# Bilinear einsum on one core: a kernel under Tile's own ordering rewritten with its own semaphores, 512-column products and row sums per unit of groups

## The chip, the cores and the metric

The kernel runs on one core of a Trainium2 chip. The metric is the device time in microseconds, taken over several executions of the kernel; lower is better. One execution was also recorded by the hardware profiler, and all times of single instructions below are from that recording, in microseconds from the start of its span.

## The reference

```python
batch, dim_i, dim_j, dim_k = 32, 256, 256, 128      # all float32
def reference(x, y, weight):
    return np.einsum('bi,bj,kij->bk', x, y, weight).astype(np.float32)
```

For each of the 128 output columns k, a 256 x 256 matrix `weight[k]` is multiplied from the left by the rows of x and from the right by the rows of y. The weight is 33.6 MB in float32 and each element of it is used once per batch row; x and y are 32 KB each, and the output is 16 KB.

## The kernel before

**Tiling.** The 128 values of k are taken as 4 (`KK`) times 32 groups (`G`), and the 256 values of i as 32 (`IP`) times 8 (`IC`). A group g holds `weight[kk*32+g]` for the four kk: 1 MB of float32. Its tile has 128 partitions, each one pair (ip, kk), and 8 x 256 columns (ic, j). The stationary operand `xblk[:, ic]` is 128 x 128: it has x for partition (ip, kk) and column (b, kk'), and zero wherever kk and kk' differ. So eight products of 256 columns, one for each ic, summed in PSUM, give the 128 rows (b, kk) of `sum_i x[b,i] weight[k,i,:]` for four k at once. VectorE then multiplies this 128 x 256 result by `y4` (y with each row repeated four times) and sums along j in the same instruction (L148), which gives one column of `acc`, 128 x 32. At the end one DMA writes `acc` to the output.

**Loads.** Group 0 is loaded in float32 by one DMA of SyncE's queue (L50, `w0`) and turned into bfloat16 by two ScalarE copies (L133). x and y are loaded by ScalarE's queue (L44, L46). Groups 1 to 31 are loaded by the POOL queue (L64), which casts float32 to bfloat16 on the way. Group 30 is loaded in two parts and group 31 in four (4, 2, 1 and 1 of the eight ic). Every load has its own tile, so no load waits for a buffer; Tile hands eight semaphores round the loads, and so from the ninth on the issue of a load waits for the landing of the one eight before it.

**Preparation.** GpSimd makes an identity matrix (L71, L72) between two loads. VectorE repeats x (L89, eight copies), TensorE transposes it (L95, eight transposes), and VectorE multiplies it by a mask (L80, L104) to make `xblk`. y is transposed by TensorE (L113), repeated by VectorE (L118), transposed back (L123) and copied to `y4` (L129).

**Order.** Tile takes the instructions of each engine in program order, adds the semaphores, and closes with a wait for everything and two barriers of all engines, with a clearing of semaphores between them. In the profile the opening barrier stands under L169 and the closing ones under L180.

Of the kernel before, what the change touches and what calls it, by code (L numbers as in the profile page):

```python
# [1 line left out]

# [4 lines left out]


@with_exitstack
def kernel(  # L10
    ctx: ExitStack,
    tc: tile.TileContext,
    x: bass.AP,
    y: bass.AP,
    weight: bass.AP,
    out: bass.AP,
):
    nc = tc.nc
    P = 128
    f32 = mybir.dt.float32  # L20
    bf16 = mybir.dt.bfloat16
    mult = mybir.AluOpType.mult
    add = mybir.AluOpType.add

    B, I = x.shape
    _, J = y.shape
    K, _, _ = weight.shape
    KK = P // B
    IP = P // KK
    IC = I // IP  # L30
    G = K // KK
    assert KK * B == P and IP * KK == P and IC * IP == I and G * KK == K

    consts = ctx.enter_context(tc.tile_pool(name="consts", bufs=1))
    wpool = ctx.enter_context(tc.tile_pool(name="wpool", bufs=1))
    psx = ctx.enter_context(tc.tile_pool(name="psx", bufs=1, space=bass.MemoryType.PSUM))
    pso = ctx.enter_context(tc.tile_pool(name="pso", bufs=4, space=bass.MemoryType.PSUM))
    tmps = ctx.enter_context(tc.tile_pool(name="tmps", bufs=2))


    w_v = weight.rearrange("(kk g) (ip ic) j -> g ip kk (ic j)", kk=KK, ic=IC)

    x_sb = consts.tile([B, I], f32)
    nc.scalar.dma_start(out=x_sb, in_=x)  # L44
    y_sb = consts.tile([B, J], f32)
    nc.scalar.dma_start(out=y_sb, in_=y)  # L46


    w0 = consts.tile([P, IC * J], f32)
    nc.sync.dma_start(out=w0, in_=w_v[0])  # L50

    def split(g):
        if g == G - 1:
            return [(0, 4), (4, 6), (6, 7), (7, 8)]
        if g == G - 2:
            return [(0, 4), (4, 8)]
        return [(0, IC)]

    w_tiles = {}

    def load(g):
        for lo, hi in split(g):
            wt = wpool.tile([P, (hi - lo) * J], bf16, name=f"w{g}_{lo}")
            nc.gpsimd.dma_start(out=wt, in_=w_v[g][:, :, lo * J:hi * J])  # L64
            for ic in range(lo, hi):
                w_tiles[g, ic] = wt[:, (ic - lo) * J:(ic - lo + 1) * J]

    load(1)

    ident = consts.tile([P, P], f32)  # L70
    nc.gpsimd.memset(ident, 0.0)  # L71
    nc.gpsimd.affine_select(  # L72
        out=ident, in_=ident, compare_op=mybir.AluOpType.not_equal, fill=1.0,
        base=0, pattern=[[-1, P]], channel_multiplier=1,
    )
    for g in range(2, G):
        load(g)

    mask = consts.tile([P, KK], f32)
    nc.vector.tensor_reduce(  # L80
        out=mask, in_=ident.rearrange("p (ip kk) -> p kk ip", kk=KK),
        axis=mybir.AxisListType.X, op=add,
    )


    x_rep = consts.tile([B, IC, IP, KK], f32)
    x_cols = x_sb.rearrange("b (ip ic) -> b ic ip", ic=IC)
    for ic in range(IC):
        nc.vector.tensor_copy(  # L89
            out=x_rep[:, ic, :, :],  # L90
            in_=x_cols[:, ic, :].unsqueeze(2).to_broadcast([B, IP, KK]),
        )
    xt_ps = psx.tile([P, IC, B], f32)
    for ic in range(IC):
        nc.tensor.transpose(  # L95
            out=xt_ps[:, ic, :],
            in_=x_rep[:, ic, :, :].rearrange("b ip kk -> b (ip kk)"),
            identity=ident[:B, :B],
        )


    xblk = consts.tile([P, IC, B, KK], bf16)
    for kk in range(KK):
        nc.vector.tensor_scalar(  # L104
            out=xblk[:, :, :, kk], in0=xt_ps, scalar1=mask[:, kk:kk + 1],
            scalar2=None, op0=mult,
        )


    JH = J // P  # L110
    yt_ps = psx.tile([P, JH, B], f32)
    for jh in range(JH):
        nc.tensor.transpose(  # L113
            out=yt_ps[:, jh, :], in_=y_sb[:, jh * P:(jh + 1) * P],
            identity=ident[:B, :B],
        )
    yt4 = consts.tile([P, JH, B, KK], f32)
    nc.vector.tensor_copy(  # L118
        out=yt4, in_=yt_ps.unsqueeze(3).to_broadcast([P, JH, B, KK])
    )  # L120
    y4_ps = psx.tile([P, J], f32)
    for jh in range(JH):
        nc.tensor.transpose(  # L123
            out=y4_ps[:, jh * P:(jh + 1) * P],
            in_=yt4[:, jh, :, :].rearrange("p b kk -> p (b kk)"),
            identity=ident,
        )
    y4 = consts.tile([P, J], f32)
    nc.vector.tensor_copy(out=y4, in_=y4_ps)  # L129

    w0b = wpool.tile([P, IC * J], bf16)
    for lo, hi in ((0, IC // 2), (IC // 2, IC)):
        nc.scalar.copy(out=w0b[:, lo * J:hi * J], in_=w0[:, lo * J:hi * J])  # L133
    for ic in range(IC):
        w_tiles[0, ic] = w0b[:, ic * J:(ic + 1) * J]

    acc = consts.tile([P, G], f32)
    for g in range(G):
        ps = pso.tile([P, J], f32)
        for ic in range(IC):  # L140
            nc.tensor.matmul(  # L141
                out=ps,
                lhsT=xblk[:, ic, :, :].rearrange("p b kk -> p (b kk)"),
                rhs=w_tiles[g, ic],
                start=(ic == 0), stop=(ic == IC - 1),
            )
        tmp = tmps.tile([P, J], f32)
        nc.vector.tensor_tensor_reduce(  # L148
            out=tmp, in0=ps, in1=y4, scale=1.0, scalar=0.0,
            op0=mult, op1=add, accum_out=acc[:, g:g + 1],  # L150
        )

    out_v = out.rearrange("b (kk g) -> b kk g", kk=KK)
    nc.sync.dma_start(out=out_v, in_=acc)


# [1 line left out]
_INS = ['x', 'y', 'weight']  # L158
_OUTS = [((32, 128), 'float32')]


# [23 lines left out]
```

## Time and profile before

| | |
|---|---|
| median of 11 runs | 88.02 us (87.87 to 88.26) |
| the profiled execution's own time | 88.03 us |
| its span, first to last instruction | 86.2 us |
| TensorE busy | 53.7 us (62%), mean granted clock 0.743 |
| VectorE busy | 18.6 us (22%) |
| GpSimd busy (nearly all of it the issue of loads) | 19.3 us (22%) |
| read from HBM | 33.62 MB, 390 GB/s over the span |

Busy time is an engine's own work; the difference between the execution's time and its span (1.8 us) lies outside the recorded instructions. PE is TensorE's matmul and PEld its loading of stationary operands. PEclk is the share of full clock that TensorE was granted. A row of the DMA queues names the queue: q0 holds the loads of the POOL queue, q1 and q10 those of SyncE and ScalarE, q8 and q14 fetches of instructions.

### The profile page before, as it was taken

Reading aid. Unit: us, or ns where it says so; the run is one execution under the profiler, and the core shown is the slowest. Engines: PE = TensorE matmul, PEld = TensorE weight load, DVE = VectorE, ACT = ScalarE, POOL = GpSimd, SP = SyncE. Lnnn points to the kernel's source line nnn. Section 1 sums busy time; section 2 is a strip of 40 time slices with the busy share of each in tenths; the row PEclk is TensorE's granted clock in tenths of the full one; section 3 lists DMA queues with packets and bytes.
Section 4 is the critical chain, followed back from the end, with each engine's and each line's share of the span. In section 5 each row is a group of like instructions: output and inputs, shape, how many; then the busy total and the mean of one; then the engine's idle time right before and its main releaser. Section 6 shows DMA issues by size and latency. Waiting matters only on the chain.

```text
span 86.2 us, 743 instructions
## 1 busy us (share of the span) xinstructions
PE 53.7 (62%) x268; PEld 32.0 (37%) x268; DVE 18.6 (22%) x79; ACT 3.3 (4%) x3; POOL 19.3 (22%) x41
## 2 busy tenths in 40 slices
PE   0517974677637882378745777378777773776360
PEld 0416643433413442234434434144443341445120
DVE  0794242022222012221130222220122222212220
ACT  2326000000000000000000000000000000000000
POOL 5980222222112221122222221122222211200000
PEclk9999999555895559755696557955555589579999
DMA  0999999999999999999999999999999999999900
GB/s 19 372 268 213 213 213 213 213 213 213 213 213 213 213 218 213 213 213 213 213 213 215 213 213 213 213 213 213 215 213 213 215 217 215 211 204 210 167 10 8
DMA packets 5427, 17.43 MB, mean 202 GB/s; under 512 B 752, under 2 KB 1200, under 8 KB 5296
## 3 DMA queue, kind: packets, MB, share of 16 engines
q0 software_dynamic: 5040, 16.26, 94.9%
q1 hardware_dynamic: 288, 1.07, 3.4%
q10 hardware_dynamic: 96, 0.07, 0.3%
q8 instruction: 2, 0.03, 0.1%
q14 instruction: 1, 0.01, 0.0%
HBM read 33.62 MB, written 0.02 MB: 390 GB/s over the span
## 4 chain that ended last, share of the span: by engine, by line
DMA 90%; issue 5%; POOL 1%; DVE 0%; PE 0%; POOLq 0%; DVEq 0%
DMA w<-in_weight_dram 90%; POOL w L64 1%; DVE tmp L148 0%; PE ps L141 0%; POOL ident L71 0%; POOLq L180 0%; POOLq L169 0%; DVEq L180 0%
## 5 line engine op out<-in xcount | busy, mean ns | idle before, releaser
L141 PE MATMUL ps<-w,xblk 128*128 128x256 bf16 x248 | 50.0, 368 | 24.4 <-DMA w<-in_weight_dram 24.3
L141 PEld LDWEIGHTS <-xblk 128*128 128x128 bf16 x256 | 30.2, 127 | 46.7 <-DMA w<-in_weight_dram 33.8
L64 POOL DMA_DIRECT2D w<-in_weight_dram x35 | 18.7, 541 | 54.3 <-DMA w<-in_weight_dram 53.5
L148 DVE CUSTOM_DVE_ANT_0 tmp<-ps,y 128x256 f32<-128x256 f32 x32 | 13.6, 425 | 61.6 <-PE ps L141 61.6
L95 PE MATMUL xt_ps<-ident,x_rep 32*128 32x32 f32 x8 | 1.2, 302 | 3.0 <-POOL ident L72 3.0
L141 PE MATMUL ps<-w0b,xblk 128*128 128x256 bf16 x8 | 2.1, 411 | 1.3 <-ACT w0b L133 1.3
L148 DVE DVE_READ_ACCUMULATOR2_ANT acc<- 128x1 f32 x32 | 2.7, 83 | 0.0
L104 DVE TENSOR_SCALAR xblk<-xt_ps,mask 128x256 bf16<-128x256 f32 x4 | 2.5, 773 | 0.1
L95 PEld LDWEIGHTS xt_ps<-ident,x_rep 32*128 32x128 f32 x8 | 1.1, 182 | 3.0 <-POOL ident L72 3.0
L133 ACT CAST w0b<-w 128x1024 bf16<-128x1024 f32 x2 | 2.0, 1043 | 3.0 <-DMA w<-in_weight_dram 3.0
L89 DVE COPY x_rep<-x_sb 32x128 f32<-32x128 f32 x8 | 1.3, 228 | 2.6 <-DMA x_sb<-in_x_dram 2.6
L133 ACT ACT_TABLE_LOAD x1 | 1.3, 1283 | 1.6 <-PEq L169 1.6
L113 PE MATMUL yt_ps<-ident,y_sb 32*128 32x32 f32 x2 | 0.4, 301 | 1.0 <-DMA y_sb<-in_y_dram 1.0
L113 PEld LDWEIGHTS yt_ps<-ident,y_sb 32*128 32x128 f32 x2 | 0.3, 200 | 1.1 <-DMA y_sb<-in_y_dram 1.1
L129 DVE COPY y<-y_ps 128x256 f32<-128x256 f32 x1 | 0.4, 425 | 1.0 <-PE y_ps L123 1.0
L123 PE MATMUL y_ps<-ident,yt 128*128 128x128 f32 x2 | 0.6, 417 | 0.0
L123 PEld LDWEIGHTS y_ps<-ident,yt 128*128 128x128 f32 x2 | 0.4, 226 | 0.1
L118 DVE COPY yt<-yt_ps 128x256 f32<-128x256 f32 x1 | 0.5, 451 | 0.0
L80 DVE TENSOR_REDUCE mask<-ident 128x4 f32<-128x128 f32 x1 | 0.4, 361 | 0.0
L72 POOL TENSOR_SCALAR_AFFINE_SELECT ident<-ident 128x128 f32<-128x128 f32 x1 | 0.3, 319 | 0.1
L71 POOL MEMSET ident<- 128x128 f32 x1 | 0.2, 224 | 0.0
L169 POOL MEMSET const-float32-0.0<- 128x1 f32 x1 | 0.1, 98 | 0.2 <-issue 0.2
(3 smaller groups left out, 0.3 us busy)
## 6 DMA issues: line engine op xcount, KB each, us to landing
w<-in_weight_dram POOLq DMA_DIRECT2D x29, 512.0 KB, 19.4
w<-in_weight_dram SPq DMA_DIRECT2D x1, 1024.0 KB, 5.1
w<-in_weight_dram POOLq DMA_DIRECT2D x3, 256.0 KB, 17.0
w<-in_weight_dram POOLq DMA_DIRECT2D x1, 128.0 KB, 14.0
w<-in_weight_dram POOLq DMA_DIRECT2D x2, 64.0 KB, 10.8
x_sb<-in_x_dram ACTq DMA_DIRECT2D x1, 32.0 KB, 1.8
y_sb<-in_y_dram ACTq DMA_DIRECT2D x1, 32.0 KB, 4.0
out_dram<-acc SPq DMA_DIRECT2D x1, 16.0 KB, 1.4
```

The costliest lines, as they stand in the source:

```text
L64: nc.gpsimd.dma_start(out=wt, in_=w_v[g][:, :, lo * J:hi * J])
L80: nc.vector.tensor_reduce(out=mask, in_=ident.rearrange("p (ip kk) -> p kk ip", kk=KK), axis=mybir.AxisListType.X, op=add,)
L89: nc.vector.tensor_copy(out=x_rep[:, ic, :, :], in_=x_cols[:, ic, :].unsqueeze(2).to_broadcast([B, IP, KK]),)
L95: nc.tensor.transpose(out=xt_ps[:, ic, :], in_=x_rep[:, ic, :, :].rearrange("b ip kk -> b (ip kk)"), identity=ident[:B, :B],)
L104: nc.vector.tensor_scalar(out=xblk[:, :, :, kk], in0=xt_ps, scalar1=mask[:, kk:kk + 1], scalar2=None, op0=mult,)
L113: nc.tensor.transpose(out=yt_ps[:, jh, :], in_=y_sb[:, jh * P:(jh + 1) * P], identity=ident[:B, :B],)
L118: nc.vector.tensor_copy(out=yt4, in_=yt_ps.unsqueeze(3).to_broadcast([P, JH, B, KK]))
L123: nc.tensor.transpose(out=y4_ps[:, jh * P:(jh + 1) * P], in_=yt4[:, jh, :, :].rearrange("p b kk -> p (b kk)"), identity=ident,)
L129: nc.vector.tensor_copy(out=y4, in_=y4_ps)
L133: nc.scalar.copy(out=w0b[:, lo * J:hi * J], in_=w0[:, lo * J:hi * J])
L141: nc.tensor.matmul(out=ps, lhsT=xblk[:, ic, :, :].rearrange("p b kk -> p (b kk)"), rhs=w_tiles[g, ic], start=(ic == 0), stop=(ic == IC - 1),)
L148: nc.vector.tensor_tensor_reduce(out=tmp, in0=ps, in1=y4, scale=1.0, scalar=0.0, op0=mult, op1=add, accum_out=acc[:, g:g + 1],)
```

## The change

Parts, in the order of the program:

- SyncE's and ScalarE's loads (`w0`, x, y) are issued inside the Tile context; then the context is closed. Its closing barriers (two of all engines, one after the other) so run at the start, behind these three issues and ahead of everything else. All further instructions are written in plain order per engine with semaphores that the kernel allocates.
- The loads of the POOL queue have a semaphore each and wait for nothing. Group 30 is one load; group 31 is still four.
- x is repeated by one copy of 1024 elements and transposed by four VectorE transposes of 32 x 32 blocks. y4 comes from one float32 product of y with `spread`, an identity with each column repeated four times.
- The 32 groups are taken in units of 8, 8, 6, 4, 3, 2 and 1. Within a unit the loop over ic is outside and the pairs of groups are inside: one product covers two groups, 512 columns, and a stationary operand is loaded once for all pairs of the unit. Units run over ic upward and downward in turn, so that a unit begins with the operand that the last one ended with.
- For each unit but the last, one VectorE multiply covers all its groups and a second instruction sums the rows. The last unit, group 31 alone, keeps the fused instruction.
- After the output's DMA has been issued, SyncE increments a semaphore on which POOL clears the others, and SyncE waits for the landing and clears the output's own. No barrier of all engines stands at the end.

```diff
+UNITS = (8, 8, 6, 4, 3, 2, 1)
+LAST = ((0, 4), (4, 6), (6, 7), (7, 8))
+BANKS = 8
...
+    for ins in (
+        nc.sync.dma_start(out=w0, in_=w_v[0]).then_inc(s_w0, 16),
+        nc.scalar.dma_start(out=x_sb, in_=x).then_inc(s_x, 16),
+        nc.scalar.dma_start(out=y_sb, in_=y).then_inc(s_y, 16),
+    ):
+        tc.no_tile_sem_insts.add(ins.ins.name)
+    tc.close()
+    tc.compile()
...
+    for g in range(1, G):
+        if g < G - 1:
+            pool.dma_start(out=w_sb[:, g, :], in_=w_v[g]).then_inc(s_w[g - 1], 16)
+        else:
+            for s, (lo, hi) in zip(s_last, LAST):
+                pool.dma_start(
+                    out=w_sb[:, g, lo * J:hi * J], in_=w_v[g][:, :, lo * J:hi * J],
+                ).then_inc(s, 16)
+        if g == 2:
+            pool.memset(ident, 0.0).then_inc(s_pool, 1)
+            pool.affine_select(
...
+    t = done(v.tensor_copy(
+        out=x_rep,
+        in_=x_sb.rearrange("b (ip ic) -> b ic ip", ic=IC).unsqueeze(3)
+        .to_broadcast([B, IC, IP, KK]),
+    )._wait_ge(s_x, 16))
+    for q in range(Q):
+        c = v.transpose(
+            out=xt[q * 32:(q + 1) * 32, :, :],
+            in_=x_rep[:, :, q * IP // Q:(q + 1) * IP // Q, :],
         )
...
+    def product(out, lhsT, rhs, first, last, load):
+        return pe.add_instruction(mybir.InstMatmult(
+            name=nc.get_next_instruction_name(), engine=mybir.EngineType.PE,
+            ins=[pe.lower_ap(rhs), pe.lower_ap(lhsT)], outs=[pe.lower_ap(out)],
+            start_tensor_calc=first, stop_tensor_calc=last,
+            tile_size=(P, P), tile_position=(0, 0), ldweights=load,
+        ))
...
+        up = (len(UNITS) - 1 - u) % 2 == 0
+        order = range(IC) if up else range(IC - 1, -1, -1)
+        for n_ic, ic in enumerate(order):
+            for b, g, n in pairs:
+                waits = []
+                if g == G - 1:
+                    waits = [s for s, (lo, _) in zip(s_last, LAST) if lo == ic]
+                elif n_ic == 0:
+                    waits = [s_w[h - 1] for h in range(max(g, 1), g + n)]
...
+                c = product(
+                    ps[:, b, :n, :], xblk[:, ic, :, :].rearrange("p b kk -> p (b kk)"),
+                    w_sb[:, g:g + n, ic * J:(ic + 1) * J],
+                    first=(n_ic == 0), last=(n_ic == IC - 1), load=(held != ic),
+                )
...
+        if n_g > 1:
+            t = done(v.tensor_tensor(
+                out=prod, in0=sums, in1=y4.unsqueeze(1).to_broadcast([P, n_g, J]), op=mult,
+            )._wait_ge(s_pe, n_pe))
+            freed[bank:bank + n_b] = [t] * n_b
+            done(v.tensor_reduce(
+                out=acc[:, g0:g0 + n_g], in_=prod, axis=AX, op=add,
+            )._wait_ge(s_dve, t))
+        else:
+            done(v.tensor_tensor_reduce(
...
+    sp.dma_start(out=out_v, in_=acc)._wait_ge(s_dve, n_dve).then_inc(s_out, 16)
+    sp.sem_inc(s_fin, 1)
+    pool.wait_ge(s_fin, 1)
+    pool.dma_reset(range(nums[0], nums[-1] + 1))
+    pool.sem_clear(range(nums[0], nums[-1] + 1))
+    sp.wait_ge(s_out, 16)
+    sp.sem_clear(s_out)
```

## The prediction

> **What bounds the kernel now.** I read the slices and the chain of the page first.
>
> ```profile
> PEclk9999999555895559755696557955555589579999
> DMA  0999999999999999999999999999999999999900
> ...
> DMA 90%; issue 5%; POOL 1%; DVE 0%; PE 0%; POOLq 0%; DVEq 0%
> ```
>
> The DMA engines are full from the second slice to the 38th, and the chain that ended last is 90% loads of the weight. Nothing that TensorE or VectorE does between slice 2 and slice 37 can be worth time; only the start (before the engines are full), the rate of the loads, and the end (from the last landing to the last instruction) can. So I looked at these three. The timeline of TensorE gives the rate, because each group of eight products starts when its load lands:
>
> ```profile
> 30.57 1.88 PE L141 MATMUL ps<-w,xblk 128*128 128x256 bf16 x8 [0.55 <-DMA w<-in_weight_dram]
> 34.00 1.05 PE L141 MATMUL ps<-w,xblk 128*128 128x256 bf16 x8 [1.55 <-DMA w<-in_weight_dram]
> 36.35 1.89 PE L141 MATMUL ps<-w,xblk 128*128 128x256 bf16 x8 [1.30 <-DMA w<-in_weight_dram]
> 38.79 1.89 PE L141 MATMUL ps<-w,xblk 128*128 128x256 bf16 x8 [0.55 <-DMA w<-in_weight_dram]
> ```
>
> Loads land 2.44 us apart (1.05 MB read in that time is 430 GB/s), except once: 3.43 us before the group at 34.00. The DMA queues between 31 and 33 us show what happened there:
>
> ```profile
> q0 software_dynamic: 115, 0.41, 102.6%
> q8 instruction: 1, 0.02, 2.9%
> ```
>
> One 16 KB packet of instructions took 2.9% of 16 engines x 2 us, 0.93 us of one engine. A load is complete when the slowest of 16 engines is. The completion increments in the trace show it: those of group 1 come from 7.86 to 8.43, 0.57 us apart; from this packet on one engine is some 1.4 us behind the first. A second such packet (0.97 us, at 71.9) puts another engine behind by 1.3 us. The increments of the last part of group 31 run from 81.76 to 83.15, and the third latest comes at 82.37: without the two packets the last load would land 0.78 us earlier. TensorE's instructions cause them: counted from its first, it has passed about 200 at 31.8 us and about 460 at 71.9, 256 apart. (The Trainium skill, "Runtime: NRT & Kernel Launch", Terms, has the instruction memory refilled in 16 KiB blocks, which are these packets.)
>
> The end, in the timeline and in the closing instructions' rows:
>
> ```profile
> 81.89 1.56 PE L141 MATMUL ps<-w,xblk 128*128 128x256 bf16 x8 [0.70 <-DMA w<-in_weight_dram]
> 83.49 0.42 DVE L148 CUSTOM_DVE_ANT_0 tmp<-ps,y 128x256 f32<-128x256 f32 x1 [1.83 <-PE ps L141]
> 83.84 0.08 DVE L148 DVE_READ_ACCUMULATOR2_ANT acc<- 128x1 f32 x1
> 83.95 0.35 SPq L154 DMA_DIRECT2D out_dram<-acc  x1
> ```
>
> ```profile
> L180 SPq EVENT_SEMAPHORE  x9: 17/28/28, 84.3 to 86.2; - x9
> L180 SPq DRAIN  x3: 7/7/13, 85.5 to 85.8; - x3
> L180 POOLq EVENT_SEMAPHORE_RANGE_CLEAR  x1: 120/120/120, 85.8 to 85.8; - x1
> ```
>
> Last landing 83.15, last product over at 83.46, row sum over at 83.92, output issued at 83.95 and landed at 85.38 (1.43 us), and then two barriers with a clearing between them to 86.25: 0.87 us in which no data moves.
>
> **The change part by part.** The sum is against the profiled execution: 88.03 us, a span of 86.25 and 1.78 outside it. Its time is within 0.01 us of the median, so no correction is needed.
>
> *Closing barriers moved to the start: -0.75 us.* At the end SyncE has left one wait and one clearing. With the price of the clearing there is (0.12 us) the end comes 0.12 us after the output's landing, in place of 0.87. POOL's own clearing is released by the output's issue, 1.43 us before its landing, and is covered by it. At the start the two barriers (each some 0.2 us by the distance of the rows above, 85.5 to 85.7 and 86.0 to 86.2) wait for ScalarE, whose issue of y ends at 1.60. So POOL's first load, issued at 1.24 before, is issued at about 2.1 to 2.7. What hides this: the engines are on `w0` from 2.15 to 5.03, and the first packet of group 1 starts on each engine just as its `w0` ends. POOL needs 0.66 us for the issue: 3.4 at the latest, 1.6 us to spare. All of VectorE's, TensorE's and ScalarE's preparation also moves 0.9 to 2 us; ScalarE waits for `w0` until 5.88 anyway, and the first products wait for group 1.
>
> *Loads without waits: 0.* POOL waits 53.5 us in 27 waits now, and the engines are never short of work meanwhile. Issuing all 34 at once (34 x 0.53 us = 18 us) only lengthens the queue. One load for group 30 in place of two saves some 0.03 us (two 2 KB packets at 0.173 us against one of 4 KB at 0.324).
>
> *Instructions: TensorE 545 to 213 by the order of the built programs.* The second fetch disappears. The first comes at about the 200th instruction, now in the last two units: some 1.2 us after group 30 has landed, when the engines have 0.5 to 1.4 us of work left. It then delays one engine by up to 0.9 us, or comes after that engine's last packet. So group 30 lands at 79.76 (now 80.56), and the last part of group 31 between 82.37 and 83.15.
>
> *Products in units.* Unit 5 (groups 29 and 30) cannot begin its second step before group 30 has landed: eight products of 512 columns. At full clock 256 columns have a pitch of 0.11 us here (eight in 1.05 with the last one's 0.28), so 512 take 0.215: 8 x 0.215 + 0.2 = 1.93, from 79.79 to 81.72. Unit 6 needs 8 x 0.11 more and then waits for its last parts: its last product ends between 82.68 and 83.46, 0.31 after the landing as now. The 206 weight loads saved are hidden now (the pitch is that of the columns alone) and bring nothing.
>
> *Row sums.* New on the path: unit 5's multiply and sum stand ahead of the last row sum on VectorE. The nearest row is L148, 425 ns for 256 elements from PSUM: 512 cost between 0.60 and 0.85; I take 0.70. For the sum, L80's 361 ns for 128 elements (read with a stride of four) bounds it at 1.44 above, L148's rate at 0.60 below; I take 0.70, since it reads without a stride. So VectorE is free at 81.75 + 0.70 + 0.05 + 0.70 = 83.20; the last row sum starts between 83.2 and 83.5, say 83.3, and is over at 83.73. **This eats most of the 0.78 us that the fetches gave back.**
>
> *Preparation of x and y: 0.* Ready at about 9 us instead of 8.4; what waits is unit 0's first step, and its second step waits for group 7 at 23 us.
>
> *Sum:* 83.73 + 0.03 to the issue + 1.43 + 0.12 = 85.31, against 86.25: -0.94. Time 88.03 - 0.94 = **87.1 us**.
>
> **Two rules of the skill weighed.** First the clock. Windows of 3.41 us, as the trace has them:
>
> ```profile
> 66.44:69.86 3.42, 2.87 (x15) 1.65 (x12) 0.43 (x2) 0.00 (x0) 0.69 (x2) 0.50 1.06 212
> 69.86:73.27 3.41, 1.36 (x11) 0.81 (x10) 0.87 (x4) 0.00 (x0) 0.53 (x1) 1.00 1.06 214
> 73.27:76.68 3.41, 2.74 (x13) 1.66 (x13) 0.43 (x2) 0.00 (x0) 0.53 (x1) 0.50 1.05 210
> 76.68:80.09 3.41, 2.17 (x17) 1.31 (x15) 0.86 (x4) 0.00 (x0) 0.00 (x0) 1.00 1.11 209
> 80.09:83.50 3.41, 2.07 (x12) 0.98 (x11) 0.44 (x3) 0.00 (x0) 0.00 (x0) 1.00 0.62 93
> ```
>
> Columns after the window: its length, busy time of PE, PEld, DVE, ACT, POOL, then the granted clock, DMA share and GB/s. Windows at half clock with 80% or more of PE busy (2.87, 2.74 of 3.41) are followed by full clock; a full window with 40% (1.36) is followed by half, one with 64% (2.17) stays full. The skill ("TensorE: Matmul & The Clock Gate", Part 1) has the clock fall only after an idle window of about 3.4 us. By the rule unit 5 runs at full clock, as I took it: the gap before it is at most 2.5 us. By the trace it may not: if unit 4 runs at full clock (done 2.6 us after group 28 lands at 74.85), a window that holds the idle rest is under 50% busy, and unit 5 gets half clock: 8 x 0.427 + 0.2 = 3.6 us, 1.7 more. Working the seven units through with these thresholds for every phase of the windows, the last row sum ends at 83.6 to 84.0 in three of four phases and at up to 84.5 in nine of ten.
>
> Second the port. Six loads issued at 2.92 took 3.25 us together, 0.54 each, the same as alone (527 ns), while VectorE's SBUF copies ran beside them (2.60 to 3.88). The skill ("SBUF — State Buffer", the trap "DVE blocks DMA") has a float32 SBUF copy of VectorE shut GpSimd out of writing descriptors until it ends. The copy of x is now one of 1024 elements, some 1.3 us (the eight took 1.28 together), beside POOL's first issue. By the trace this costs nothing; by the rule the issue ends at 4.7 and the spare time of 1.6 us shrinks to 0.3, still nothing, unless descriptors need longer than that to reach the engines.
>
> **The rivals.**
> (A) *Slower: half clock in unit 5.* Place: the eight products after group 30's landing. Price 1.7 us on VectorE's start if it holds throughout: last row sum over at 85.4, time 88.8. It turns the change into a loss once it costs over 1.15 us, that is, when 2.3 of the 3.6 us run at half. For it: TensorE now works in bursts with gaps. Against: unit 4 mostly begins at half clock and fills a window before unit 5.
> (B) *Group 1 late.* If its descriptors became ready only just before 5.03, the 0.9 to 1.4 us of delay leave the engines idle, and everything after moves by up to 0.9: 87.1 to 88.0. For it: no packet of group 1 runs between `w0`'s, though y's do. Against: 3.1 us from the end of that issue to its first packet is long against ScalarE's x (0.65).
> (C) *The closing does not count.* What the barriers did is paid outside the span instead: -0.2 only, 87.85. Against: the 1.78 us outside are already there with barriers.
> (D) *The fetch misses and VectorE is quicker than taken:* last row sum from 82.9, time 86.7.
>
> **How the numbers follow.** The plain case with (D) at its lower edge has 0.66: 86.7 to 87.6, all faster. (A) has 0.18; in about half of it the loss is under 0.7 us (faster still), in the rest it makes 0.02 same and 0.08 slower, up to 88.8. (B) 0.08: 0.03 faster, 0.04 same, 0.01 slower. (C) 0.08: 0.04, 0.03, 0.01. Together 0.81 faster, 0.09 same, 0.10 slower; about 0.2% (0.18 us) is what a measurement of this kernel can tell. The range from 86.7 to 88.1 leaves out the slower cases and little below.
>
> **What would show it.** Right: q8 with one packet at most, near 81; group 30's products starting near 79.8; the output's issue near 83.75; SyncE's last instruction some 0.1 us after its landing; POOL's first load at 2.1 to 2.7 with the DMA row still full. Wrong: PEclk 0.5 in the last two slices with the output issued after 84.5; a gap of the DMA share near 5 us; a difference of time and span well above 1.8; a rate of loads other than 2.44 us.

## The result: 87.2 us in place of 88.1

| | before | changed kernel | the same kernel, later |
|---|---|---|---|
| median (range), runs | 88.09 us (87.72 to 88.28), 47 | 87.21 us (86.44 to 87.90), 12 | 86.99 us (86.14 to 87.89), 6 |
| ratio to before, 95% interval | | 0.9884 [0.9865, 0.9902] | 0.9841 [0.98, 0.9881] |
| profiled execution: time, span | 88.03, 86.25 | 87.90, 86.37 | 86.71, 85.40 |
| time less span | 1.73 to 1.86 | 1.27 to 1.36 in nine runs; 1.5, 1.5 and 2.3 | 1.29 to 1.47 |

The forecast was 87.1 us. A ratio here leaves out a run more than 1.5% above the fastest of its kernel, and for the changed kernel these are late runs of the kind that this text is about, so the median of all runs stands beside each ratio. The changed kernel spreads over 1.5 to 1.75 us where the one before spreads over 0.56. Its first profile shows an execution at the upper end, the second (called after-again below) one in the middle; both are needed.

Slices and chain of the page, first profile:

```profile
PEclk9999999999999999955555999975999659999859
DMA  0999999999999999999999999999999999999900
...
DMA 50%; PE 21%; POOL 14%; another core or an unknown queue 9%; issue 1%; DVE 1%; POOLq 0%
```

The DMA row is the one of before: full from the second slice to the 38th. The chain fell from 90% DMA to 50%, and that is no sign of a new bound. The chain steps back to what released an instruction or, where nothing did, to the one ahead of it on its engine. The products now run in bursts of up to 32, and POOL's issues wait for nothing, so it walks through them. The rate of the loads is the same: from group 1 to group 29 the first completion increments are 2.46 us apart in the mean in both kernels.

The start, in the timeline (first us, then duration):

```profile
2.42 0.68 DVE L126 COPY x_rep<-x_sb 32x1024 f32<-32x1024 f32 x1 [2.42 <-PEq L89]
2.87 1.21 POOL L96 DMA_DIRECT2D w_sb<-in_weight_dram  x2 [2.42 <-POOLq L89]
```

POOL's first load is issued 1.6 us later than before, at 2.87, because the barriers of L89 end for POOL at 2.27, where before the opening barrier (L169) ended at 0.64; from there it is 0.60 us to the issue in both kernels. (The 2.42 in these brackets is how long the engine sat idle.) Group 1's first packet comes at 5.09, as `w0`'s last packets run out: no gap in the DMA row.

The end of the first profile, in the timelines of TensorE, VectorE and SyncE:

```profile
80.16 4.26 PE L166 MATMUL ps<-w_sb,xblk 128*128 128x512 bf16 x16 [2.39 <-DMA w_sb<-in_weight_dram]
...
82.75 0.69 DVE L216 TENSOR_TENSOR tmp<-ps,y 128x512 f32<-128x512 f32 x1 [3.00 <-PE ps L166]
83.47 0.69 DVE L220 TENSOR_REDUCE acc<-tmp 128x2 f32<-128x512 f32 x1
84.45 0.42 DVE L224 CUSTOM_DVE_ANT_0 tmp<-ps,y 128x256 f32<-128x256 f32 x1 [0.29 <-PE ps L166]
...
84.92 0.34 SPq L233 DMA_DIRECT2D out_dram<-acc  x1
```

and of after-again:

```profile
79.72 2.32 PE L166 MATMUL ps<-w_sb,xblk 128*128 128x512 bf16 x12 [0.74 <-DMA w_sb<-in_weight_dram]
82.82 0.61 PE L166 MATMUL ps<-w_sb,xblk 128*128 128x256 bf16 x4 [0.78 <-DMA w_sb<-in_weight_dram]
...
81.65 0.69 DVE L216 TENSOR_TENSOR tmp<-ps,y 128x512 f32<-128x512 f32 x1 [0.68 <-PE ps L166]
82.37 0.69 DVE L220 TENSOR_REDUCE acc<-tmp 128x2 f32<-128x512 f32 x1
83.47 0.42 DVE L224 CUSTOM_DVE_ANT_0 tmp<-ps,y 128x256 f32<-128x256 f32 x1 [0.41 <-PE ps L166]
...
83.93 0.34 SPq L233 DMA_DIRECT2D out_dram<-acc  x1
```

From unit 5's first product, which waits for group 30, to VectorE's multiply it is 2.59 us in the first and 1.93 in the second. The windows of TensorE's granted clock (window, its length, busy time of PE, PEld, DVE, ACT, POOL, then the clock, DMA share, GB/s) say why. First profile, then after-again:

```profile
77.81:81.23 3.42, 1.07 (x5) 0.48 (x5) 1.91 (x2) 0.00 (x0) 0.00 (x0) 1.00 1.10 201
81.23:84.64 3.41, 3.19 (x12) 1.36 (x9) 1.56 (x3) 0.00 (x0) 0.00 (x0) 0.50 0.23 30
```

```profile
75.28:78.69 3.41, 3.41 (x12) 0.76 (x5) 0.00 (x0) 0.00 (x0) 0.00 (x0) 0.50 1.08 217
78.69:82.10 3.41, 2.62 (x14) 0.97 (x10) 2.37 (x3) 0.00 (x0) 0.00 (x0) 1.00 1.02 170
```

In the first, a window at full clock was busy for 31% of its time, and the next one, which holds the last products, was granted half clock. In after-again unit 4 ran at half clock, filled its window, and unit 5 got full clock.

This can be followed through all 14 profiles of this text, window by window. Of the full-clock windows, each of the 46 in which TensorE was busy for 41% or less was followed by half clock, and each of the 88 with 47% or more by full clock; the four between went either way. After half clock, 76% or less kept it (42 windows) and 80% or more gave full clock (44 windows). The place of the windows in the program differs from run to run, so the same kernel can fall on either side.

So after-again compares like with like against before: 85.40 against 86.25 us of span.

In after-again one fetch of instructions comes at 80.72, 1.04 us after group 30 has landed (DMA queues, 80 to 82 us), and SyncE's last instruction is this:

```profile
q0 software_dynamic: 458, 0.31, 104.1%
q8 instruction: 1, 0.02, 3.0%
```

```profile
L239 SPq EVENT_SEMAPHORE_RANGE_CLEAR  x1: 25/25/25, 85.4 to 85.4; - x1
```

The packet (0.97 us) puts one engine 1.6 us behind the first, and the last part lands at 83.09. In the first profile no packet lies in the span and the last part lands at 82.71. The output lands at 85.36 in after-again and the span ends 0.04 us later, against 0.87 before.

### The profile page after: what moved, and what is told of

Same layout as the page of the kernel before. It is cut to its first block, busy times and chain, and to the rows that moved or that the text cites. A ratio compares the mean times of both kernels' runs of the same rounds, so it can differ in the third digit from the quotient of the medians.

```text
span 86.4 us, 323 instructions
## 1 busy us (share of the span) xinstructions
PE 39.5 (46%) x138; PEld 6.3 (7%) x52; DVE 23.4 (27%) x26; ACT 3.3 (4%) x3; POOL 19.9 (23%) x40
## 4 chain that ended last, share of the span: by engine, by line
DMA 50%; PE 21%; POOL 14%; another core or an unknown queue 9%; issue 1%; DVE 1%; POOLq 0%
DMA w_sb<-in_weight_dram 50%; PE ps L166 21%; POOL w_sb L96 13%; DVE tmp L224 0%; POOL ident L104 0%; POOL ident L103 0%; POOLq L89 0%; DVE acc L224 0%
## 5 line engine op out<-in xcount | busy, mean ns | idle before, releaser
L166 PE MATMUL ps<-w_sb,xblk 128*128 128x512 bf16 (+1 forms) x136 | 38.3, 441 | 39.7 <-DMA w_sb<-in_weight_dram 39.7
L216 DVE TENSOR_TENSOR tmp<-ps,y 128x2048 f32<-128x2048 f32 (+4 forms) x6 | 9.2, 1536 | 58.4 <-PE ps L166 58.4
L96 POOL DMA_DIRECT2D w_sb<-in_weight_dram x30 | 17.1, 775 | 2.4 <-POOLq L89 2.4
L166 PEld LDWEIGHTS ps<-w_sb,xblk 128*128 128x128 bf16 x50 | 5.8, 116 | 72.4 <-issue 68.3
L220 DVE TENSOR_REDUCE acc<-tmp 128x8 f32<-128x2048 f32 (+4 forms) x6 | 9.2, 1531 | 0.2
L157 PE MATMUL ps<-y_sb,spread 32*128 32x256 f32 x2 | 1.2, 706 | 5.3 <-DVE spread L139 5.3
L99 POOL DMA_DIRECT2D w_sb<-in_weight_dram x4 | 2.6, 1061 | 0.0
L112 ACT CAST w_sb<-w 128x1024 bf16<-128x1024 f32 x2 | 2.0, 1044 | 2.2 <-DMA w<-in_weight_dram 2.2
L132 DVE STREAM_TRANSPOSE xt<-x_rep 32x256 f32<-32x256 f32 x4 | 1.7, 435 | 0.1
L147 DVE TENSOR_SCALAR xblk<-xt,mask 128x256 bf16<-128x256 f32 x4 | 1.4, 499 | 0.0
L224 DVE CUSTOM_DVE_ANT_0 tmp<-ps,y 128x256 f32<-128x256 f32 x1 | 0.4, 424 | 0.3 <-PE ps L166 0.3
L104 POOL TENSOR_SCALAR_AFFINE_SELECT ident<-ident 128x128 f32<-128x128 f32 x1 | 0.3, 287 | 0.1
```

Source lines behind the costliest of these rows:

```text
L96: pool.dma_start(out=w_sb[:, g, :], in_=w_v[g]).then_inc(s_w[g - 1], 16)
L99: pool.dma_start(out=w_sb[:, g, lo * J:hi * J], in_=w_v[g][:, :, lo * J:hi * J],).then_inc(s, 16)
L112: c = act.copy(out=w_sb[:, 0, lo:hi], in_=w0[:, lo:hi])
L132: c = v.transpose(out=xt[q * 32:(q + 1) * 32, :, :], in_=x_rep[:, :, q * IP // Q:(q + 1) * IP // Q, :],)
L147: c = v.tensor_scalar(out=xblk[:, :, :, kk], in0=xt, scalar1=mask[:, kk:kk + 1], scalar2=None, op0=mult,)
L157: pe.matmul(out=ps[:, BANKS - 1, 0, :], lhsT=spread.rearrange("p b kk -> p (b kk)"), rhs=y_sb, start=True, stop=True,)._wait_ge(s_dve, t_s ...
```

## The experiments

The theory at this point: the gain is the closing (0.83 us of span) and what lies outside the span (0.47 us in most runs, not foreseen); what units and row sums add at the end eats what the vanished fetch gives; the spread is TensorE's clock in unit 5. The rivals: the gain is the missing fetch; it is the larger products; it is the loads without waits. The before runs beside the three groups of kernels had medians of 88.02, 88.16 and 88.06 us.

**1. The changed kernel again**, with no edit.

> The changed kernel itself, as the measure for the other runs beside it. Theory: the saving of 0.9 us is 0.8 us of closing barriers and about 0.7 us of earlier landings, minus 0.5 to 1.5 us lost behind group 30 to the clock and to VectorE's pair of instructions. Expected 87.2 us median, runs spread over more than 1 us, since the phase of the clock's windows differs from run to run; before 88.1 with a spread of 0.5.

Measured: 86.99 us (6 runs), the column above. The size of the gain repeats, and so does the spread: spans from 84.8 to 86.6.

**2. The closing of before, put back** at the end (the barriers at the start stay).

```diff
-    sp.sem_inc(s_fin, 1)
-    pool.wait_ge(s_fin, 1)
-    pool.dma_reset(range(nums[0], nums[-1] + 1))
-    pool.sem_clear(range(nums[0], nums[-1] + 1))
     sp.wait_ge(s_out, 16)
-    sp.sem_clear(s_out)
+    nc.all_engine_barrier()
+    pool.dma_reset(range(nums[0], s_out.num + 1))
+    pool.sem_clear(range(nums[0], s_out.num + 1))
+    nc.all_engine_barrier()
```

> The changed kernel with the closing of the kernel before put back (wait for the output, barrier of all engines, clearing, barrier). If the closing barriers were worth what the rows of before say, the span grows by 0.7 to 0.85 us and the time by the same, to 88.0. If their cost is paid outside the span anyway (the rival that the closing does not count), the time stays at 87.2 and the difference of time and span falls from 1.5 to about 0.8.

Measured: 89.72 us (88.59 to 90.74, 6 runs), ratio 1.0138 [1.0092, 1.0184]: with this one part undone, the changed kernel is slower than before. In its profile the output lands at 86.62 and the span ends at 87.61, 0.99 us later. The rows of the two barriers (durations min/median/max, first and last start):

```profile
L236 POOLq EVENT_SEMAPHORE  x2: 17/17/17, 86.7 to 86.8; - x2
...
L239 POOLq EVENT_SEMAPHORE  x2: 17/17/17, 87.4 to 87.5; - x2
L239 SPq EVENT_SEMAPHORE  x1: 17/17/17, 87.5 to 87.5; - x1
```

Time less span also grew, to 2.1 in two runs and 2.8 to 3.3 in four. So the time is 1.7 us above the forecast of 88.0. In the profiled run (3.1) a fetch comes at 90.0 us, after the span. Hence experiment 5.

**3. The fetches put back**: TensorE passes 660 more waits, all long fulfilled, ahead of its first product. Two go into one instruction, so it has 543 instructions (before: 545).

```diff
+    for _ in range(660):
+        pe.wait_ge(s_y, 16)
     pe.wait_ge(s_dve, t_x)
```

> The changed kernel with 330 more instructions on TensorE's queue (waits that are fulfilled already) ahead of the first product, 543 in all instead of 213. Theory: two 16 KB packets of instructions come back on queue q8, each puts one engine 0.85 us behind, group 30 and the last part of group 31 land 0.4 to 0.8 us later and the time grows by as much, to 87.6 to 88.0. Rival: the late landings are hidden by VectorE's queue at the end, and the time moves by less than 0.2. The waits themselves last 20 us at the start, when TensorE has nothing to do before group 7 lands at 23 us; what they delay in unit 0 has 20 us to catch up.

Measured: 87.15 us (87.05 to 88.79, 6 runs), ratio 0.9897 [0.9877, 0.9916]. Two packets are back, as at 31 and 72 us before. The DMA queues from 29 to 31 us have this line:

```profile
q8 instruction: 1, 0.02, 2.9%
```

The second is at 69.58 us, and two engines end 1.4 us behind the first. Group 30 lands at 80.53 in place of 79.68, the last part at 83.13, and the output is issued at 84.28. Five spans are 85.7 to 85.9, against 84.8 for the fastest run of the unpadded kernel and 84.72 in the profile of experiment 9, whose packet does no harm. That is some 0.9 us for two packets, as was thought; against after-again's profile, where one packet holds the last part back, it is 0.35.

But the time was forecast at 87.6 to 88.0, and the median moved by 0.16 us, which is what the rival said. That the dearer packets are made up for by fewer runs with half clock in unit 5 fits the profile (full clock there, after a window that was 56% busy) and the five runs within 0.2 us of each other; for the runs without a profile it is an inference. The sixth run, 88.79, is not explained.

TensorE's mean clock, 0.94 to 0.98 here and 0.84 to 0.88 without the waits, must not be read as a faster clock:

```profile
41.22 16.53 PE L166 MATMUL ps<-w_sb,xblk 128*128 128x512 bf16 x66 [34.73 <-issue]
```

The waits hold the first product back until 41.22 us, 34.7 us and not 20. The mean counts this idle time as full clock. Then TensorE works off what has landed without a gap until 57.75, and those windows stay full.

**4. Unit 5's row sums as two fused ones** instead of a multiply and a sum.

```diff
-        if n_g > 1:
+        if n_g > 2:
...
+            for h in range(n_g):
+                c = v.tensor_tensor_reduce(
+                    out=fused[:, g0 + h - (G - 4), :], in0=sums[:, h, :], in1=y4, scale=1.0, scalar=0.0,
```

> The changed kernel with the fused multiply and sum (one instruction for each group) for unit 5 too, instead of one multiply and one sum over both groups. Theory: unit 5 takes 2 x 0.43 = 0.9 us on VectorE in place of 0.69 + 0.03 + 0.69 = 1.41, so where TensorE is at full clock the last row sum starts 0.4 us earlier: 86.8. Rival, that TensorE and not VectorE is what is last: no change, which is what should be seen in the runs with half clock in unit 5.

Measured: 86.89 us (85.95 to 87.52, 6 runs), ratio 0.9833 [0.9788, 0.9879], not to be told from after-again. VectorE is free at 82.63, 0.43 us earlier than in after-again. But a fetch came at 80.71 here too, the last part landed at 83.13, and the last row sum began at 83.50. What VectorE gives back goes into its wait for the last landing whenever the fetch comes there.

**5. Both: the fetches and the closing of before.**

> Both edits at once: the 330 instructions on TensorE's queue ahead of the products, and the closing of the kernel before. end_barriers cost 2.7 us instead of 0.8, and its time stands 2.1 to 3.3 us above its span; in its profile a packet of instructions is fetched after the span's end, at 90.0. Theory: that fetch is a miss at the end, and not the barriers' price. With the fetches moved into the loads, the closing costs 0.95 in the span (as end_barriers showed) and time minus span goes from 1.31 to the 1.8 of the kernel before: 87.1 + 1.4 = 88.5, with a small spread. Rival, that barriers themselves cost 2.7 here: 89.8.

Measured: 89.49 us (88.68 to 90.73, 6 runs), ratio 1.0115 [1.0066, 1.0164]. The output lands at 87.08 and the span ends at 88.07: 0.99 us again. Time less span is 2.0 to 2.1 in all six runs. So against experiment 3 (0.04 and some 1.3) the closing costs 0.95 us in the span and 0.7 outside it; the further 0.8 to 1.3 us in four runs of experiment 2 are gone together with the late fetch. That the late fetch makes them is only argued. (Experiment 11 has a second case: its profiled run, with a fetch 1.3 us behind the span, has 1.97 us outside, the other four 1.29 to 1.45.)

The total, 89.49 us, misses the forecast of 88.5 and the small spread, and as a number lies nearer to the rival's 89.8; only the two parts above, each read by itself, speak for 1.65 us and not 2.7. The remaining 0.7 of the 2.34 us between the medians is put down to half clock. The profile has it from 81.68 on, with the multiply 2.74 us after unit 5's first product in place of 1.92 in experiment 3, and the fastest span, 86.6, is just 0.9 above that of experiment 3; for the other runs it is an inference.

**6. The 512-column products alone**, in the kernel before (groups 0 to 29 in pairs, fused row sums group by group; 319 TensorE instructions).

```diff
+    for h in range(G // 2 - 1):
+        ps = pso.tile([P, 2, J], f32, name="ps2")
...
+                rhs=pair[h][:, :, ic * J:(ic + 1) * J],
```

> The kernel before with one part of the change alone, under Tile: products of 512 columns over pairs of groups (0 to 29), groups 30 and 31 as they were, the fused row sums and everything else as before. TensorE has 319 instructions in place of 545. Theory: the products themselves are hidden, so only the fetches count: one packet in place of two, which leaves one engine 0.9 us behind, so little is gained (one of the two late engines is enough): 87.6 to 88.0. If the fetch should fall before or behind the loads: 87.3. Rival, that wider products are worth time by themselves: below 87.2.

Measured: 88.25 us (87.9 to 88.8, 12 runs), ratio 1.0015 [0.9994, 1.0035]. The forecast was 87.6 to 88.0; nothing was gained. One fetch packet is left, but it comes at 80.86, and the last part lands at 83.24 as before. Fewer and larger products bring nothing by themselves, and fewer fetches bring nothing if the one left falls on the last load.

**7. One semaphore for each pair of loads**, which takes 11 waiting instructions off TensorE (213 to 202).

```diff
-            pool.dma_start(out=w_sb[:, g, :], in_=w_v[g]).then_inc(s_w[g - 1], 16)
+            pool.dma_start(out=w_sb[:, g, :], in_=w_v[g]).then_inc(of[g][0], 16)
...
-                    waits = [s_w[h - 1] for h in range(max(g, 1), g + n)]
+                    waits = [of[g]]
```

> The changed kernel with one semaphore for the two loads of a pair of groups, so that the extra wait instructions go: TensorE has 202 instructions in place of 213. In two profiles of the changed kernel a packet of instructions came 1.1 us after group 30 landed and held the last parts of group 31 back by 0.8 us. Theory: the packet is asked for at a fixed place of the instruction stream, which now is 11 instructions later, in the middle of the last unit, whose products wait for the last parts: it comes at 81.5 to 82.5, when the engines are through or nearly. The last part lands near 82.3 instead of 83.1 and the time falls by 0.2 (VectorE is free at 83.1 only) to 86.7. Rival, that the packet comes anyhow at some 1 us after group 30: no change, 87.0.

Measured: 86.82 us (86.05 to 88.1, 6 runs), ratio 0.9807 [0.9755, 0.986]. The profile has no fetch in the span, the last part landed at 82.49. Four spans are 84.7 to 85.0; two are 86.2 and 86.8, and the profile of the latter has half clock from 79.96 on, after a window that was about 30% busy, with the output issued at 85.32:

```profile
79.94 4.44 PE L175 MATMUL ps<-w_sb,xblk 128*128 128x512 bf16 x16 [2.41 <-DMA w_sb<-in_weight_dram]
...
83.54 0.69 DVE L223 TENSOR_TENSOR tmp<-ps,y 128x512 f32<-128x512 f32 x1 [4.04 <-PE ps L175]
...
85.32 0.35 SPq L240 DMA_DIRECT2D out_dram<-acc  x1
```

Here half clock holds for all of unit 5, and from its first product to the multiply it is 3.60 us (3.57 in the profile of experiment 2). One run has 2.5 us outside its span; that stays unexplained.

**8. Units 8, 8, 6, 4, 3, 1, 1, 1** in place of 8, 8, 6, 4, 3, 2, 1, with the fused row sum for units of one.

```diff
-UNITS = (8, 8, 6, 4, 3, 2, 1)
+UNITS = (8, 8, 6, 4, 3, 1, 1, 1)
```

> The changed kernel with units 8, 8, 6, 4, 3, 1, 1, 1: groups 29 and 30 each alone with a fused row sum. After group 30's landing there are then eight products of 256 columns (1.05 us at full clock, 1.9 at half) in place of eight of 512 (1.9 and 3.6), and one row sum of 0.43 on VectorE in place of 1.4. Theory: the half clock costs at most 0.85 us here and the spread of the runs falls to 0.5 us or less; but with 227 instructions the packet of instructions now comes before group 30 has landed and holds one engine back by 0.9, so the last part lands at 83.1 to 83.2: 86.7, the fastest runs no faster than before. Rival, that the clock has nothing to do with the spread: it stays above 1 us.

Measured: 86.92 us (86.71 to 87.12, 6 runs), ratio 0.9866 [0.9836, 0.9896]. The spread falls to 0.41 us. TensorE's timeline shows group 30's own eight products at full clock:

```profile
80.55 1.03 PE L167 MATMUL ps<-w_sb,xblk 128*128 128x256 bf16 x8 [2.24 <-DMA w_sb<-in_weight_dram]
81.80 1.63 PE L167 MATMUL ps<-w_sb,xblk 128*128 128x256 bf16 x8 [0.22 <-DMA w_sb<-in_weight_dram]
```

But the kernel has 227 instructions, its fetch came at 78.18, early enough to hold up group 30 (80.50) as well as the last part (83.11), and the fastest runs are lost. With the last part that late in the profile, there is also less for a half clock to delay, so this experiment alone does not show how much of the smaller spread is the small units' doing.

**9. Experiments 7 and 4 together.**

> shared_sems with the fused row sums for unit 5 (202 instructions on TensorE). fused_pair showed no difference, since in its profile the packet of instructions held the last part back to 83.1, when VectorE was free anyway. Theory: where no packet comes, VectorE's pair of instructions for unit 5 is last (free at 83.1, last landing 82.4), so the fused ones save 0.3 to 0.4 us: fastest spans 84.4 in place of 84.7, median 86.5. Rival: TensorE's products are last even then: no change against shared_sems (86.8).

Measured: 87.06 us (85.97 to 87.45, 6 runs), ratio 0.9808 [0.9766, 0.985]. In its profile the fetch (81.61) is too late to do harm: last part at 82.37, last row sum at 82.79, output issued at 83.25, span 84.72. The forecast was a fastest span of 84.4 and a median of 86.5; the fastest spans are those of experiment 7, as the rival said. VectorE is free at 82.69 and the last product is over at 82.75, so fusing the row sums is worth nothing in either case.

**10. Experiments 7 and 8 together** (217 instructions).

> units_3111 with one semaphore for a pair of loads, 217 instructions on TensorE in place of 227. Theory: the small units remove the spread that the clock makes; if the packet of instructions moves behind group 30 as it did with 213 instructions, it still hits the loads of group 31, and the time stays at 86.7 to 86.9; if it misses them the last part lands at 82.4 and the time is 86.1.

Measured: 86.88 us (86.86 to 87.13, 4 runs), ratio 0.987 [0.9854, 0.9886]. Spread 0.27 us; the fetch at 80.86, the last part at 83.23.

**11. Units 8, 8, 8, 4, 2, 1, 1** with experiment 7 and fused row sums for units of one and two (202 instructions).

```diff
-UNITS = (8, 8, 6, 4, 3, 2, 1)
+UNITS = (8, 8, 8, 4, 2, 1, 1)
```

> The version that the runs point to: units 8, 8, 8, 4, 2, 1, 1, shared semaphores, fused row sums for units of one or two; 202 instructions on TensorE, as many as shared_sems, whose fast runs had no packet within the loads. After group 30 there are only eight products of 256 columns and one row sum. Theory: last part at 82.4, last row sum over at 83.2, span 84.7, and no spread by the clock: 86.1, with all runs below 86.5. Rival: a packet comes in spite of the count: 86.8.

Measured: **86.19 us (86.03 to 86.65, 5 runs), ratio 0.9798 [0.9776, 0.9821]**, the best version of all by the median (its interval lies below that of experiment 12, run beside it, and below the first one of the changed kernel; it overlaps those of after-again and of experiments 4, 7 and 9, from which late runs are left out). Its windows and its end (timeline):

```profile
72.77:76.18 3.41, 3.05 (x15) 0.59 (x6) 2.79 (x3) 0.00 (x0) 0.00 (x0) 1.00 1.07 216
76.18:79.59 3.41, 1.89 (x8) 0.68 (x7) 2.45 (x3) 0.00 (x0) 0.00 (x0) 1.00 1.04 206
79.59:83.01 3.42, 2.55 (x16) 1.27 (x14) 1.13 (x7) 0.00 (x0) 0.00 (x0) 1.00 0.80 128
```

```profile
79.83 1.03 PE L176 MATMUL ps<-w_sb,xblk 128*128 128x256 bf16 x8 [0.61 <-DMA w_sb<-in_weight_dram]
...
81.05 1.67 PE L176 MATMUL ps<-w_sb,xblk 128*128 128x256 bf16 x8 [0.18 <-DMA w_sb<-in_weight_dram]
...
82.75 0.42 DVE L233 CUSTOM_DVE_ANT_0 fused<-ps,y 128x256 f32<-128x256 f32 x1 [1.42 <-PE ps L176]
...
83.22 0.34 SPq L246 DMA_DIRECT2D out_dram<-acc  x1
```

Unit 4 of two groups ends later than one of three, so the window ahead of group 30's products is 55% busy (1.89 of 3.41) and the clock stays full through the last product. Group 30's products take 1.03 us. The fetch comes at 85.97, behind the span, and the last part lands at 82.39, so the output is issued 0.71 us earlier than in after-again. None of the five spans reaches 86 us, against two of six in experiments 7 and 9 each; with so few runs and one profile, that every place of the windows spares this version is not shown.

**12. The waits of the loads put back**, so that at most eight whole groups are queued.

```diff
     for g in range(1, G):
+        if g > 8:
+            pool.wait_ge(s_w[g - 9], 16)
```

> The changed kernel with the waits of the kernel before put back on POOL's queue: the issue of each load from the ninth on waits for the landing of the one eight before it. Theory: no change, 87.0 to 87.2 with the same spread, since the engines are never short of queued work either way. Rival, that issuing all loads at once (the last ones take 1.06 us in place of 0.53 to issue) slows or speeds the loads: the landings, 2.46 us apart now, move to 2.44 or less and the time by 0.6 us.

Measured: 86.95 us (86.61 to 87.8, 6 runs), ratio 0.9884 [0.9847, 0.9922], no change. The costliest groups show the waits back on POOL, and the landings stay 2.46 us apart:

```profile
L98 POOL DMA_DIRECT2D w_sb<-in_weight_dram x30 | 16.8, 567 | 43.0 <-DMA w_sb<-in_weight_dram 40.5
```

## Why the prediction was right, point by point

The number was right (87.1 against 87.21 and 86.99), and in part by luck, because two misses cancel: 0.47 us outside the span that no step had, and half clock in unit 5, which the sum left out and which many runs have. For a run without it the sum itself was close: a span of 85.31 against 85.40 in after-again, with the output issued 0.17 us later and the closing 0.08 us shorter than forecast.

*Closing, predicted -0.75:* right, and a little small. The end comes 0.04 us after the landing, not 0.12 (the last clearing takes 25 ns, not 120), so -0.83. Experiments 2 and 5 give 0.95 when it is put back.

*Rival C, the closing is paid outside the span:* wrong in sign. The sum held time less span at 1.78; it fell to 1.31, **a gain of 0.47 us that no step had.** Experiment 5 shows that barriers at the end also cost 0.7 us outside the span. What happens there no trace shows.

*Fetches:* the second packet did disappear. The first came where predicted, 1.04 us after group 30's landing, in after-again, and not within the span in the first profile: last part at 83.09 and 82.71, inside the predicted 82.37 to 83.15. Group 30 landed at 79.68 (predicted 79.76) in after-again and at 80.11 in the first profile, where one engine is 0.9 us behind from group 1 on, without a packet. Experiment 3 prices the two packets at some 0.9 us of span. The reason given for their places, 256 TensorE instructions from one to the next, holds only roughly: counted by the instructions begun, they come at 200 and 459 before and at 234 and 471 in experiment 3. The first comes at 286 in experiment 6 and at 187 to 202 in the profiles of experiments 4 and 8 to 11 and of after-again, while the same program as after-again had none in the first profile. What sets the place stays open.

*Products and row sums:* unit 5 at full clock took 1.93 us (predicted 1.93), the multiply 0.69 and the sum 0.69 (0.70 each, the nearest rows having been L148's and L80's). The output was issued at 83.93 with the fetch (predicted 83.76).

*Rival A, half clock in unit 5, held at 0.18:* **the step that was mis-sized, by its chance and not by its price.** It is in the first profile and in those of experiments 2, 5, 7 and 12, five of the nine with this unit 5. Of the 18 runs of the changed kernel seven have spans of 86.0 or more, close to the first profile's 86.37; that they all had half clock is an inference from the profiles. Its price was set at 1.7 us if half clock holds throughout (3.6 us for 1.93), and where it does, in experiments 2 and 7, 3.57 and 3.60 were measured; in experiment 7 the last row sum is over at 85.29 (forecast 85.4). In the first profile half clock began at 81.23, with the first five of unit 5's products done, and cost 0.66 us of the 0.99 by which its output is issued later than in after-again. Another 0.44 is group 30's later start, which is the lagging DMA engine's doing, and 0.12 comes off because after-again waits longer for its last landing than the first profile for its last products. So an engine that lags is a second reason for late runs, and the runs without a profile do not tell the two apart.

A late run still ends ahead of before, or near it: the first profile's span is 0.12 us longer than before's, but what lies outside is 0.25 shorter (1.53 against 1.78). Without the gain outside, the median would be at 87.7. The limit for a loss, 1.15 us, does not follow from the sum, which gives 1.04: the 0.94 won, and 0.1 for which VectorE waits.

*The two rules weighed.* By the Trainium skill ("TensorE: Matmul & The Clock Gate", Part 1) the clock falls only after an idle window. The window from 77.81 to 81.23 was 31% busy, TensorE's longest gap in it was 2.39 us, and half clock followed: the trace's reading was right (all 14 profiles bear it out), and I should have let it decide the middle of the forecast and not only its edge. For the port ("SBUF — State Buffer", "DVE blocks DMA") the copy of x is no test: it took 0.68 us and not 1.3, and POOL's first issue overlaps its last 0.23 us only; that issue took 0.67 us, as before (0.66). A stall like the one that the page describes came elsewhere, at the four multiplies by the mask:

```profile
4.61 4.57 POOL L96 DMA_DIRECT2D w_sb<-in_weight_dram  x7
...
5.53 1.37 DVE L147 TENSOR_SCALAR xblk<-xt,mask 128x256 bf16<-128x256 f32 x4
```

Of these seven issues the third, begun at 5.67, is recorded for 1.35 us in place of 0.55. It ends at 7.02, 0.12 us after the last multiply, and this holds in all 12 profiles with these multiplies: they end between 6.90 and 7.01, and the issue 0.12 to 0.13 later. Before, the multiplies (L104) read PSUM and not SBUF, and no issue is held. That the port is the cause is inferred from these times. The change brought this stall in, and the prediction had not looked for it; it cost nothing, because four loads were queued by then.

*Loads without waits, 0:* right (experiment 12). *Preparation and group 1 (rival B):* no gap at 5.09, although POOL's issue came 0.17 us after the latest predicted time.

What the whole comes to: of the 1.0 us between before and the changed kernel's later runs, 0.83 is the closing in the span and 0.47 lies outside it; that leaves 0.3 us which the rest of the change, the units with their row sums and the fetch they save, gives back. This remainder was not measured by itself: in after-again's profile, without half clock, it is nothing (a span shorter by 0.85), so it stands for the late runs. Experiment 11 turns it into a gain with shaped last units and the fetch behind the span together; neither alone did it (experiments 10 and 7).

## What to carry to other kernels

Where loads fill the DMA engines from start to end, look at what comes after the last byte: closing barriers cost 0.95 us of span and 0.7 outside it in experiment 5 (0.83 and 0.47 were won by moving them), more than everything done to 34 loads, 136 products and their sums. Larger units save instructions but put more work behind the last landings and leave TensorE idle in between; shrink the last units so that what follows a landing is one load's products, and keep the window ahead of them busy enough for full clock (47% of 3.41 us always sufficed in these profiles, 41% never did). A packet of instructions takes 0.95 us of one of 16 engines, and a load is as late as its slowest engine: where it falls matters more than how many there are.

## What had not been expected of the hardware

- Time outside the span is not a constant: 1.73 to 1.86 us with one set of closing barriers, 1.27 to 1.36 in most runs without, 2.0 to 2.1 with barriers at both ends, and 1.97 and 3.1 in the two profiled runs with a fetch after the end.
- The recorded time of POOL's issues grows with what is queued, from 0.55 us to 1.09 for the last of 34, but the issues still begin 0.52 us apart; the records overlap, and POOL is not slowed. With the waits of experiment 12 most take 0.53.
- VectorE's multiplies from SBUF hold one of POOL's issues for 0.8 us, until 0.12 us after the last of them; the same multiplies from PSUM do not.
- A mean clock counts time without products as full clock: 0.94 to 0.98 in experiment 3, where TensorE's first product comes at 41.22 us.
- One DMA engine can be 0.9 us behind from the first load on with no packet to show for it (the first profile), and stays so to the last.
